# The delta rule's triangular inverse as 128-wide block diagonal matrices, and an mLSTM walk with zero padded operands

## The chip, the core and the metric

The kernel runs on one core of a Trainium2 chip. TensorE multiplies matrices, VectorE, ScalarE and GpSimd work on the results, and SyncE issues the DMAs. Measured is the device time of one execution, in microseconds; lower is better.

## The reference

One layer of a hybrid decoder, for a prompt of 256 tokens and 8 samples of one token each, with d_model 2048, all in fp32. An input projection of x feeds four mixers side by side: a gated delta rule (A, 8 heads), a Conformer convolution of width 31 (B), a short gated convolution (C) and an mLSTM matrix memory (D, 4 heads). Each is projected, gated and merged; then come an output projection, a cross-attention and a squared-ReLU MLP of 8192. What the change touches are the two recurrences, which run over the prompt in four chunks of 64 tokens:

```
# A, per chunk and head (L = 64)
a_low = where(strict, beta_i * (k k^T) * decay, 0)
sol   = triangular_solve(I + a_low, [v*beta, k*beta*exp(gc)])   # u, w
delta = u - w S;  o = q_dec S + (q k^T * decay) delta;  S = S*g_last + k_dec^T delta
# D, per chunk and head
dmat = exp(log_d - m_tok) * (q k^T)
num  = inter * (q C) + dmat v;  den = inter * (q n) + sum(dmat)
h    = num / max(|den|, exp(-m_tok))
C, n = scale * C + (k*wgt)^T v,  scale * n + k^T wgt
```

## The kernel before

Most of the work is weight matmuls. Every weight comes as blocks of 128x1024 (`raw`), is split into a high part `wh` (ScalarE) and a low part `wl` (VectorE, every second to fourth block GpSimd), and multiplied as wh*xh + wh*xl + wl*xh into `g` (L320). One block with its 24 matmuls is a *slot*; `run()` (L289) walks over all slots, feeds the blocks two slots ahead, and between slots pays out steps of two lists of generators: at most one step of `chain` (the delta units, row stage, mLSTM units) per slot and as many of `fill` (the convolution of B, 30 products per column block) as an estimate of VectorE's time, `dv_t` (L116), leaves room for. The order of instructions within each engine is settled when the program is built, by a scheduler with a timeline of its own.

The delta rule runs as four units of two heads (`a_unit`, L676). A unit normalises q and k, forms for four chunks and two heads the matrices A (strictly lower, scaled) and its transpose, and inverts I + A by doubling: T and U hold the inverse and its transpose for diagonal blocks of 2, and in five levels (L802, blocks of 2, 4, 8, 16, 32) X, minus the product of A and U, is formed in `xb`, evicted by ScalarE into `m_dl`, multiplied by T into `ub` and by the transpose into `tb`, and taken over by VectorE through a mask (`copy_predicated`, L818 and L821). Two chunks lie one above the other on the 128 partitions, each 64x64; `each()` (L655) issues eight 64x64 matmuls per product, which use a quarter of the array each. After the levels GpSimd copies U into the diagonal blocks of a zeroed 128x128 tile `UB` (L827), and the walk over the four chunks multiplies with that (`db`, `ob`, `sb`, `ks`, L844). Beside the levels, `side(li)` issues transposes and the sample part.

The mLSTM runs as two units of two heads (`d_unit`, L1074). Its walk (L1202) adds into one bank `nb` the product of the queries with C and that of the 64x64 matrices `QK` with v, head 0 in the output's lower 64 partitions and head 1 in the upper, and forms the update of C in `cb` from 64 rows of `kw` and v. The columns are 256 of v and one of ones, 257.

A matmul of fp32 operands shows as two records in the trace, one of fp32r operands (the weight matmuls) and a transpose as one.

Of the kernel before, what the change touches and what calls it, by code (L numbers as in the profile page):

```python
# [36 lines left out]
HP = 0  # L37
SCRATCH = 8192
DELAY = 3
# [52 lines left out]
def decoder_step(ctx, tc, A, O):  # L92
# [29 lines left out]
    def act(out, in_, func, bias=0.0, scale=1.0, **kw):  # L122
        return AC.activation(out, in_, func, bias=bias, scale=scale, **kw)  # L123

    def tt(out, a, b, op, eng=None):
        if eng is None:
            cost(out)
        return (eng or DV).tensor_tensor(out=out, in0=a, in1=b, op=op)  # L128

    def ts(out, a, s1, op0, s2=None, op1=None):  # L130
        cost(out, 0.6)
        if op1 is None:
            DV.tensor_scalar(out, a, s1, None, op0=op0)
        else:
            DV.tensor_scalar(out, a, s1, s2, op0=op0, op1=op1)
# [41 lines left out]
    cst = cp.tile([P, NCC], F32, name="cst")  # L177
    mint = cp.tile([P, 2, len(LEVELS), CH], mybir.dt.uint8, name="mint")
    oner = cp.tile([P, P], F32R, name="ones")
# [56 lines left out]
    def dma(dst, src):  # L236
        after(SP.dma_start(dst, src), "SP")
# [196 lines left out]
    selw = w1.tile([P, 8, P], F32R, name="selw")  # L434
    UB = w1.tile([P, 2, 2, P], F32, name="UB")
    dlz = [w1.tile([P, 2, P], F32, name="dl%d" % i) for i in range(2)]
    c1 = w1.tile([P, 2, 4, 8], F32, name="c1")
# [6 lines left out]
    GP.tensor_copy(RD[:].rearrange("p f l -> p (f l)"), zero[:].to_broadcast([P, 2 * CH]))  # L444
    GP.memset(UB[:], 0.0)
    for t in dlz:
        GP.memset(t[:], 0.0)
    rown = [0]
    nm = 2 * len(LEVELS) * CH
    w3 = rowt[:, 13:16, :]  # L450
    mf = w3.rearrange("p a b -> p (a b)")[:, 0:nm]

    ws = rowt[:, 4:6, :].rearrange("p a b -> p (a b)")[:, 0:32 * KB]

    def loads():
        dma(pc[:], A["pc"])
        dma(ws, A["ws"].rearrange("p k c -> p (k c)"))
        dma(cst[:], A["cst"])
        dma(mf, A["mint"].rearrange("p a b c -> p (a b c)"))
        win_a(0)  # L460
        win_b(0)
        dma(winC[:], A["sC"])
        dma(m0[rD, :], A["m0"])
# [16 lines left out]
    def row_stage():  # L480
        cp1, cp2 = rtile("cp1", NP), rtile("cp2", NP)
        GP.memset(cp1[:], 0.0)
        GP.memset(cp2[:], 0.0)
        cpy(mint[:].rearrange("p a b c -> p (a b c)"), mf)
        GP.memset(w3[:, 0, NP:], 0.0)
# [202 lines left out]
    def a_unit(u):  # L688
# [17 lines left out]
        sh = [P, 2, 2, CH]  # L706
        dL, dT = mat("m_dl"), mat("m_dt")
        Am, T, U = (mat("m_" + n) for n in ("a", "t", "u"))
        QK, X = dT, dL
        tt(dL[:], Gs[0], colb(c1, 1, h0, 2, sh), SUB)  # L710
        ts(dT[:], dL[:], 0.0, MIN)
        ts(dL[:], dL[:], 0.0, MAX)
        act(dT[:], dT[:], AF.Exp)
        act(dL[:], dL[:], AF.Exp, scale=-1.0)
        tt(U[:], KQ[:, :, :, 1, :], dT[:], MUL)
        tt(Am[:], KQ[:, :, :, 1, :], dL[:], MUL)
        tt(U[:], U[:], Gs[1], MUL)
        tt(dT[:], dT[:], con("incl")[:, None, None, :].to_broadcast(sh), MUL, eng=GP)
        tt(QK[:], KQ[:, :, :, 0, :], dT[:], MUL)
        yield  # L720
        tt(Am[:], Am[:], colb(c1, 0, h0, 2, sh), MUL)
        for dst, src, m in ((U, U, "m1u"), (T, Am, "m1t")):
            tt(dst[:], src[:], con(m)[:, None, None, :].to_broadcast(sh), MUL)
            tt(dst[:], dst[:], con("eye")[:, None, None, :].to_broadcast(sh), ADD)
        yield
        sv = [P, 2, 2, P]
        v5 = lambda b: b[:].rearrange("p (f h l) -> p f h l", f=2, h=2)
        vt, kd = (w1.tile(sv, F32, tag=n, name=n) for n in ("vt", "kd"))

        st = {}  # L730

        def side(li):
# [9 lines left out]
            if li == 1:  # L742
                kb = bank("kb")
                for i in range(4):
                    PE.transpose(kb[:, i * P:(i + 1) * P], k[:, i % 2, (i // 2) * P:(i // 2 + 1) * P], ident)
                tt(kd[:], v5(kb), colb(c1, 2, h0, 2, sv), MUL)
            if li == 2:
# [54 lines left out]
        for li, s in enumerate(LEVELS):  # L802
            last = li == len(LEVELS) - 1
            xb = v4(bank("xb"))
            for hf, hh, o, t in each():
                mm(xb[o, hf, hh], Am[o, hf, hh], U[o, hf, hh])
            act(X[:], xb, AF.Copy, scale=-1.0)
            side(li)
            yield
            ub = v4(bank("ub"))  # L810
            tb = None if last else v4(bank("tb"))
            for hf, hh, o, t in each():
                mm(ub[o, hf, hh], T[o, hf, hh], X[o, hf, hh])
            if not last:
                for hf, hh, o, t in each():
                    mm(tb[o, hf, hh], X[o, hf, hh], T[o, hf, hh])
            cost(U[:])
            DV.copy_predicated(U[:], mint[:, 0, li, None, None, :].to_broadcast(sh), ub)  # L818
            if not last:
                cost(T[:])  # L820
                DV.copy_predicated(T[:], mint[:, 1, li, None, None, :].to_broadcast(sh), tb)  # L821
            yield

        side(5)
        for c in range(2):
            o = slice(CH * c, CH * c + CH)
            GP.tensor_copy(UB[o, :, :, o], U[o])  # L827
        yield
# [18 lines left out]
        for c in range(NCH):  # L847
# [11 lines left out]
            for hh in range(2):  # L859
                mm(db[:, hh], UB[:, hf, hh], vt[:, hf, hh])  # L860
            act(dl[o], db[o], AF.Copy)
# [213 lines left out]
    def d_unit(u):  # L1075
# [3 lines left out]
        sh = [P, 2, 2, CH]  # L1079
        KQ = v4(bank("KQd"))  # L1080
# [3 lines left out]
        for hf, hh, o, t in each():  # L1084
            mm(KQ[o, hf, hh], k[:, hh, t], q[:, hh, t])
        E, QK = mat("m_dl"), mat("m_dt")
# [4 lines left out]
        tt(QK[:], KQ, E[:], MUL)  # L1091
        yield
# [11 lines left out]
        sv = [P, 2, 2, P]  # L1104
        kw = w1.tile(sv, F32, tag="kw", name="kwD")
        tt(kw[:], kb[:].rearrange("p (f h l) -> p f h l", f=2, h=2), colb(c2, 3, h0, 2, sv), MUL)
        yield
# [6 lines left out]
        for hh in range(2):  # L1114
            mm(ib[:, hh], sel(8 + h0 + hh, P), RR[:, 1, 0:NP])
        qi = q[:, :, 0:NP]
        tt(qi, q[:, :, 0:NP], ib, MUL)
        sl = w1.tile([P, 2, NCH], F32, tag="gl", name="sl")
# [83 lines left out]
        for c in range(NCH):  # L1202
            hf, o = c // 2, slice(CH * (c % 2), CH * (c % 2) + CH)
            t = slice(c * CH, c * CH + CH)
# [540 lines left out]
def _prep(i):  # L1745
# [43 lines left out]
    rst[:, ::CH] = 0.0  # L1789
    a["cst"] = np.concatenate([np.eye(P, dtype=f), (pl == j).astype(f), (pl <= j).astype(f), -up.astype(f), -lo.astype(f), rst], 1)  # L1790
    mi = np.zeros((P, 2, len(LEVELS), CH), np.float32)
    for n, s in enumerate(LEVELS):
        same = pl // (2 * s) == j // (2 * s)
        mi[:, 0, n] = same & (pl // s % 2 == 0) & (j // s % 2 == 1)
        mi[:, 1, n] = same & (pl // s % 2 == 1) & (j // s % 2 == 0)
    a["mint"] = mi
# [60 lines left out]
```

## Time and profile before

| | us |
|---|---|
| three runs | 2353.32, 2354.43, 2358.15 |
| median | 2354.43 |
| the profiled execution | 2356.15 |
| its span, first to last instruction | 2354.4 |

In the profile, "PE g L150" is a matmul into `g` recorded at line 150, the helper `mm`; PEld is the loading of its weights, DVE is VectorE, ACT ScalarE, POOL GpSimd. A shape such as "64*64 64x64" is the weights' rows and columns and the output's partitions and columns. A matmul's length in the timeline includes its way through the array, so that records overlap; what a stream costs is read from start to start. The rows of a timeline merge equal records ("x16") and show in brackets what the engine waited for.

### The profile page before, as it was taken

Reading aid. Unit: us, or ns where it says so; the run is one execution under the profiler, and the core shown is the slowest. Engines: PE = TensorE matmul, PEld = TensorE weight load, DVE = VectorE, ACT = ScalarE, POOL = GpSimd, SP = SyncE. Lnnn points to the kernel's source line nnn. Section 1 sums busy time; section 2 is a strip of 40 time slices with the busy share of each in tenths; the row PEclk is TensorE's granted clock in tenths of the full one; section 3 lists DMA queues with packets and bytes.
Section 4 is the critical chain, followed back from the end, with each engine's and each line's share of the span. In section 5 each row is a group of like instructions: output and inputs, shape, how many; then the busy total and the mean of one; then the engine's idle time right before and its main releaser. Section 6 shows DMA issues by size and latency. Waiting matters only on the chain.

```text
span 2354.4 us, 46439 instructions
## 1 busy us (share of the span) xinstructions
PE 2254.9 (96%) x19034; PEld 2210.5 (94%) x19034; DVE 1269.0 (54%) x2039; ACT 1166.9 (50%) x1789; POOL 978.9 (42%) x741
## 2 busy tenths in 40 slices
PE   9869999989999999999989999999999999999997
PEld 8869998988999999999989998889999999999997
DVE  7968899786446445443364466476323323323323
ACT  5735556545455455444434455456435534534543
POOL 3524435332122223343343355256445544544576
PEclk9989999999999999999999999999999999999998
DMA  6685555574566666766556666645666555556553
GB/s 228 161 121 169 168 168 163 162 136 146 176 185 194 185 217 201 226 193 181 180 181 180 190 204 196 202 145 156 180 180 179 179 180 179 179 180 180 179 180 126
DMA packets 140398, 418.78 MB, mean 178 GB/s; under 512 B 31896, under 2 KB 36248, under 8 KB 140184
## 3 DMA queue, kind: packets, MB, share of 16 engines
q1 hardware_dynamic: 140184, 415.80, 59.9%
q8 instruction: 149, 2.44, 0.4%
q14 instruction: 65, 0.53, 0.1%
HBM read 402.32 MB, written 14.38 MB: 177 GB/s over the span
## 4 chain that ended last, share of the span: by engine, by line
PE 77%; DVE 13%; DMA 5%; ACT 2%; issue 2%; POOL 1%; SPq 0%; DVEq 0%; POOLq 0%; ACTq 0%
PE g L150 70%; DVE wl L128 3%; DVE cB L139 3%; DMA raw<-in_win_dram 2%; DVE cu L139 2%; PE q L150 1%; DVE y L128 1%; PE pv L150 1%; DMA dbc<-dd 1%; ACT wh L123 1%; DMA mr<-in_memT_dram 1%; DVE y L139 1%; DMA raw<-in_winq_dram 1%; DVE s L139 0%; PE cb L150 0%
## 5 line engine op out<-in xcount | busy, mean ns | idle before, releaser
L123 ACT ACTIVATE wh<-raw 128x1024 fp32r<-128x1024 f32 (+1 forms) x705 | 745.3, 1058 | 850.3 <-PE g L150 283.1
L128 POOL TENSOR_TENSOR wl<-raw,wh 128x1024 fp32r<-128x1024 f32 x240 | 588.6, 2453 | 724.5 <-PE g L150 513.1
L150 PE MATMUL g<-xh,wl 128*128 128x264 f32 x2496 | 715.0, 287 | 11.4 <-DVE wl L128 8.8
L128 DVE TENSOR_TENSOR wl<-raw,wh 128x1024 fp32r<-128x1024 f32 (+1 forms) x465 | 588.5, 1266 | 253.0 <-PE g L150 166.7
L150 PE MATMUL g<-xh,wh 128*128 128x264 f32 x2496 | 717.6, 288 | 4.1 <-ACT wh L123 4.1
L150 PE MATMUL g<-xl,wh 128*128 128x264 f32 x2496 | 717.9, 288 | 1.3 <-issue 1.3
L150 PEld LDWEIGHTS g<-xh,wl 128*128 128x128 f32 x2496 | 473.9, 190 | 15.2 <-DVE wl L128 10.0
L150 PEld LDWEIGHTS g<-xh,wh 128*128 128x128 f32 x2496 | 474.4, 190 | 9.0 <-ACT wh L123 4.8
L150 PEld LDWEIGHTS g<-xl,wh 128*128 128x128 f32 x2496 | 473.1, 190 | 2.4 <-issue 1.5
L150 PE MATMUL g<-hgl,wh 128*128 128x264 f32 x1024 | 290.6, 284 | 0.0
L150 PE MATMUL g<-hgh,wl 128*128 128x264 f32 x1024 | 290.3, 284 | 0.0
L150 PE MATMUL g<-hgh,wh 128*128 128x264 f32 x1024 | 289.4, 283 | 0.0
L150 PE MATMUL g<-zh,wh 128*128 128x266 f32 x960 | 275.8, 287 | 2.4 <-DVE zw L128 2.4
L150 PE MATMUL g<-zl,wh 128*128 128x266 f32 x960 | 275.3, 287 | 0.0
L150 PE MATMUL g<-zh,wl 128*128 128x266 f32 x960 | 275.1, 287 | 0.0
L150 PEld LDWEIGHTS g<-hgl,wh 128*128 128x128 f32 x1024 | 192.9, 188 | 0.0
L150 PEld LDWEIGHTS g<-hgh,wh 128*128 128x128 f32 x1024 | 192.7, 188 | 0.0
L150 PEld LDWEIGHTS g<-hgh,wl 128*128 128x128 f32 x1024 | 192.0, 188 | 0.0
L150 PEld LDWEIGHTS g<-zh,wh 128*128 128x128 f32 x960 | 182.1, 190 | 2.5 <-ACT wh L123 2.5
L128 DVE TENSOR_TENSOR y<-y,g 128x264 f32<-128x264 f32 x80 | 34.3, 429 | 277.1 <-PE g L150 277.1
L150 PEld LDWEIGHTS g<-zl,wh 128*128 128x128 f32 x960 | 182.4, 190 | 0.0
L150 PEld LDWEIGHTS g<-zh,wl 128*128 128x128 f32 x960 | 181.6, 189 | 0.0
(482 smaller groups left out, 3453.5 us busy)
## 6 DMA issues: line engine op xcount, KB each, us to landing
raw<-in_win_dram SPq DMA_DIRECT2D x312, 512.0 KB, 4.1
raw<-in_f_dram SPq DMA_DIRECT2D x248, 512.0 KB, 4.2
raw<-in_wbr_dram SPq DMA_DIRECT2D x64, 512.0 KB, 3.7
raw<-in_wout_dram SPq DMA_DIRECT2D x32, 512.0 KB, 4.5
s<-in_sS_dram SPq DMA_DIRECT2D x8, 512.0 KB, 5.6
dbc<-dd SPq DMA_DIRECT2D x16, 256.0 KB, 3.7
out_S_s_dram<-s SPq DMA_DIRECT2D x8, 512.0 KB, 5.1
c<-in_sCm_dram SPq DMA_DIRECT2D x8, 512.0 KB, 5.3
```

The source lines that it names most:

```text
L123: return AC.activation(out, in_, func, bias=bias, scale=scale, **kw)
L128: return (eng or DV).tensor_tensor(out=out, in0=a, in1=b, op=op)
L139: return DV.scalar_tensor_tensor(out=out, in0=a, scalar=s, in1=b, op0=op0, op1=op1)
L150: PE.matmul(out, lhsT, rhs, start=start, stop=stop)
```

## The change

All matrices of the inverse (A, T, U, X) become 128x128 per pair of chunks, with the two 64x64 matrices on the diagonal and zeros beside them, in one tile `inv` that lives through all units; each product is four 128x128 matmuls instead of eight 64x64 ones. U is then multiplied directly, and UB and its copies go. The masks are twice as wide and come as bytes, without the cast. In the mLSTM, `KQd` is formed for whole 128-token pairs, `QK`, `qi` and `kw` are written into zeroed parts of `inv` and a tile `walk` (in every row 64 zeros, then the other head's 64 columns), so that each matmul of the walk uses 128 rows and writes 128 output partitions, and both heads add into the same bank.

```diff
-    UB = w1.tile([P, 2, 2, P], F32, name="UB")
-    dlz = [w1.tile([P, 2, P], F32, name="dl%d" % i) for i in range(2)]
+    inv = w1.tile([P, 4, 2, 2, P], F32, name="inv")
+    walk = w1.tile([P, 4, 2, P], F32, name="walk")
+    Am, T, U, X = (inv[:, i] for i in range(4))
+    dlz = [walk[:, 2 + i] for i in range(2)]
...
-        dma(mf, A["mint"].rearrange("p a b c -> p (a b c)"))
+        dma(mint[:], A["mint"])
...
-        cpy(mint[:].rearrange("p a b c -> p (a b c)"), mf)
... a_unit
-        tt(Am[:], Am[:], colb(c1, 0, h0, 2, sh), MUL)
-        for dst, src, m in ((U, U, "m1u"), (T, Am, "m1t")):
-            tt(dst[:], src[:], con(m)[:, None, None, :].to_broadcast(sh), MUL)
-            tt(dst[:], dst[:], con("eye")[:, None, None, :].to_broadcast(sh), ADD)
+        for c in range(2):
+            o = slice(CH * c, CH * c + CH)
+            tt(Am[o, :, :, o], Ah[o], colb(c1[o], 0, h0, 2, [CH, 2, 2, CH]), MUL)
+        sb = [P, 4, P]
+        f4 = lambda t: t.rearrange("p f h l -> p (f h) l")
+        Uv = f4(Uh)[:, :, None, :].to_broadcast([P, 4, 2, CH])
+        tt(f4(U).rearrange("p g (s l) -> p g s l", s=2), Uv,
+           con("m1u").rearrange("p (s l) -> p s l", s=2)[:, None].to_broadcast([P, 4, 2, CH]), MUL)
+        tt(f4(T), f4(Am), con("m1t")[:, None, :].to_broadcast(sb), MUL)
+        for t in (U, T):
+            tt(f4(t), f4(t), ident[:, None, :].to_broadcast(sb), ADD)
...
-            xb = v4(bank("xb"))
-            for hf, hh, o, t in each():
-                mm(xb[o, hf, hh], Am[o, hf, hh], U[o, hf, hh])
-            act(X[:], xb, AF.Copy, scale=-1.0)
+            xb = v5(bank("xb"))
+            for hf, hh in pairs:
+                mm(xb[:, hf, hh], Am[:, hf, hh], U[:, hf, hh])
+            act(X, xb, AF.Copy, scale=-1.0)
...
-            for hf, hh, o, t in each():
-                mm(ub[o, hf, hh], T[o, hf, hh], X[o, hf, hh])
+            for hf, hh in pairs:
+                mm(ub[:, hf, hh], T[:, hf, hh], X[:, hf, hh])
...
-            DV.copy_predicated(U[:], mint[:, 0, li, None, None, :].to_broadcast(sh), ub)
+            DV.copy_predicated(U, mint[:, 0, li, None, None, :].to_broadcast(sv), ub)
...
-        for c in range(2):
-            o = slice(CH * c, CH * c + CH)
-            GP.tensor_copy(UB[o, :, :, o], U[o])
...
-                mm(db[:, hh], UB[:, hf, hh], vt[:, hf, hh])
+                mm(db[:, hh], U[:, hf, hh], vt[:, hf, hh])
... d_begin
+            GP.memset(inv[:, 0:2], 0.0)
+            GP.memset(inv[:, 2:4], 0.0)
+            GP.memset(walk[:], 0.0)
... d_unit
-        for hf, hh, o, t in each():
-            mm(KQ[o, hf, hh], k[:, hh, t], q[:, hh, t])
+        for hf in range(2):
+            for hh in range(2):
+                t = slice(hf * P, hf * P + P)
+                mm(KQ[:, hf, hh], k[:, hh, t], q[:, hh, t])
...
-                    mm(nb[64 * hh:64 * hh + 64, :257], qi[:, hh, t], C[:, hh, :], stop=False)
+                    mm(nb[:, :257], qi[:, c, CH * hh:CH * hh + P], C[:, hh, :], start=hh == 0, stop=False)
             for hh in range(2):
-                mm(nb[64 * hh:64 * hh + 64, :257], QK[o, hf, hh], vt[o, hf, hh, :], start=c == 0)
+                mm(nb[:, :257], QK[:, hf, c % 2, CH * hh:CH * hh + P], vt[:, hf, hh, :], start=c == 0 and hh == 0, stop=hh == 1)
...
-                mm(cbs[hh], kw[o, hf, hh], vt[o, hf, hh])
+                mm(cbs[hh], kw[:, hf, c % 2, hh], vt[:, hf, hh])
```

On TensorE, in the first delta unit, the second level before, between the weight matmuls `g` (`kb` are transposes of `side`; `m_a`, `m_u`, `m_dl`, `m_t` are A, U, X and T):

```order
L150 MATMUL g<-xl,wh 128x264
L150 MATMUL xb<-m_u,m_a 64x64 x8
L745 MATMUL kb<-cst,qkv 128x128 x4
L150 MATMUL g<-xh,wl 128x264
...
L150 MATMUL g<-xh,wh 128x264
L150 MATMUL ub<-m_dl,m_t 64x64 x8
L150 MATMUL tb<-m_t,m_dl 64x64 x8
L150 MATMUL g<-xl,wh 128x264
```

The same level now, with all four matrices in `inv`:

```order
L150 MATMUL g<-xh,wh 128x264
L150 MATMUL xb<-inv 128x128 x4
L753 MATMUL kb<-cst,qkv 128x128 x4
L150 MATMUL g<-xl,wh 128x264
...
L150 MATMUL g<-xh,wh 128x264
L150 MATMUL ub<-inv 128x128 x4
L150 MATMUL tb<-inv 128x128 x4
L150 MATMUL g<-xl,wh 128x264
```

Half as many matmuls of four times the area stand at the same place; no weight matmul moves between them.

On TensorE, the second chunk of the first mLSTM unit's walk before (`hb` transposes the chunk before it, `C` is the matrix memory):

```order
L150 MATMUL g<-xh,wl 128x264
L1236 MATMUL hb<-cst,hs 128x128 x2
L150 MATMUL nb<-C,qkvD 64x257 x2
L150 MATMUL nb<-vtD,m_dt 64x257 x2
L150 MATMUL cb<-vtD,kwD 128x257 x2
L150 MATMUL g<-xh,wh 128x264
```

and now:

```order
L150 MATMUL g<-xh,wl 128x264
L1253 MATMUL hb<-cst,hs 128x128 x2
L150 MATMUL nb<-C,walk 128x257 x2
L150 MATMUL nb<-vtD,inv 128x257 x2
L150 MATMUL cb<-vtD,inv 128x257 x2
L150 MATMUL g<-xh,wh 128x264
```

The number of matmuls and their place are the same; the two products into `nb` have 128 output partitions instead of 64.

On ScalarE, in the first delta unit, an eviction of X between the weight blocks before (`cB`, `ht` and `cuC` belong to the two convolutions):

```order
L123 ACTIVATE cB<-extB,pc 128x256
L123 ACTIVATE ht<-g,pc 128x264
L123 ACTIVATE wh<-raw 128x1024 x2
L123 ACTIVATE m_dl<-xb 128x256
L123 ACTIVATE wh<-raw 128x1024
L123 ACTIVATE cuC<-extC,pc 128x256
```

and now:

```order
L123 ACTIVATE cB<-extB,pc 128x256
L123 ACTIVATE ht<-g,pc 128x264
L123 ACTIVATE wh<-raw 128x1024 x2
L123 ACTIVATE inv<-xb 128x512
L123 ACTIVATE wh<-raw 128x1024
L123 ACTIVATE cuC<-extC,pc 128x256
```

It is the eviction of the third level before and of the second now; it stands behind the same two weight blocks, and is twice as wide.

## Rows read from the trace of the kernel before

**Rows 1.** The page: busy us (share of span) and instructions by engine

```profile
PE 2254.9 (96%) x19034; PEld 2210.5 (94%) x19034; DVE 1269.0 (54%) x2039; ACT 1166.9 (50%) x1789; POOL 978.9 (42%) x741
```

**Rows 2.** Two stretches: PE, PEld, DVE, ACT, POOL busy us, clock, DMA share, GB/s

```profile
150.00:500.00 350.00, 334.76 (x3142) 324.85 (x3140) 310.86 (x550) 189.11 (x344) 143.78 (x177) 1.00 0.54 165
...
640.00:1200.00 560.00, 560.00 (x4592) 545.32 (x4591) 267.49 (x419) 272.56 (x392) 167.30 (x96) 1.00 0.64 194
```

**Rows 3.** TensorE's timeline, fourth unit, first level: start, length, instruction

```profile
553.74 0.28 PE L150 MATMUL g<-xh,wh 128*128 128x264 f32 x1
553.95 0.68 PE L150 MATMUL ub<-m_dl,m_t 64*64 64x64 f32 x16
554.47 0.63 PE L150 MATMUL tb<-m_t,m_dl 64*64 64x64 f32 x16
555.03 0.39 PE L150 MATMUL g<-xl,wh 128*128 128x264 f32 x1
555.25 0.28 PE L150 MATMUL g<-xh,wl 128*128 128x264 f32 x1
```

**Rows 4.** The same timeline, last level of the first unit

```profile
175.62 0.28 PE L150 MATMUL g<-xh,wh 128*128 128x264 f32 x1
175.84 0.68 PE L150 MATMUL ub<-m_dl,m_t 64*64 64x64 f32 x16
...
176.67 0.28 PE L150 MATMUL g<-xh,wl 128*128 128x264 f32 x1
```

**Rows 5.** The same timeline, ks of the fourth unit

```profile
595.47 0.28 PE L150 MATMUL g<-pairC,wh 128*128 128x264 f32 x1
595.59 0.61 PE L150 MATMUL ks<-S,qkv 128*128 128x128 f32 x4
...
596.16 0.29 PE L150 MATMUL g<-pairC,wl 128*128 128x264 f32 x1
```

**Rows 6.** The same timeline, second chunk of the first mLSTM unit

```profile
825.02 0.28 PE L150 MATMUL g<-xh,wl 128*128 128x264 f32 x1
...
825.45 0.65 PE L150 MATMUL nb<-C,qkvD 128*64 128x257 f32 x4
826.03 0.65 PE L150 MATMUL nb<-vtD,m_dt 64*64 64x257 f32 x4
826.62 1.13 PE L150 MATMUL cb<-vtD,kwD 64*128 64x257 f32 x4
...
827.91 0.29 PE L150 MATMUL g<-xl,wh 128*128 128x264 f32 x1
```

**Rows 7.** The same timeline, attention product of 256 columns

```profile
1542.78 0.28 PE L150 MATMUL gxo<-ox,wl 128*128 128x264 f32 x1
1542.90 1.46 PE L150 MATMUL av<-att 128*128 128x256 f32 x6
...
1544.44 0.29 PE L150 MATMUL gxo<-ox,wl 128*128 128x264 f32 x1
```

**Rows 8.** VectorE's groups, 50 to 600 us: count, busy us, mean ns, idle before

```profile
L818 DVE COPY_PREDICATED m_u<-mint,ub 128x256 f32<-128x256 uint8 x20 | 8.9, 443 | 6.5 <-PE ub L150 6.5
...
L128 DVE TENSOR_TENSOR vt<-vb,c 128x512 f32<-128x512 f32 x4 | 2.7, 682 | 0.6 <-PE vb L740 0.6
...
L128 DVE TENSOR_TENSOR m_t<-m_t,cst 128x256 f32<-128x256 f32 x4 | 1.7, 413 | 0.0
```

**Rows 9.** GpSimd's groups: a memset

```profile
L445 POOL MEMSET UB<- 128x512 f32 x1 | 0.5, 524 | 0.0
```

**Rows 10.** The page: what the DMA engines moved

```profile
DMA packets 140398, 418.78 MB, mean 178 GB/s; under 512 B 31896, under 2 KB 36248, under 8 KB 140184
```

**Rows 11.** TensorE's waits, 100 to 600 us: total, times, longest

```profile
PE ub L150 <- ACT m_dl L123: 15.7, 1, 15.7
PE ssl2q L150 <- ACT sql2q L123: 4.2, 2, 2.6
...
PE ssl2q L150 <- POOL sql2q L128: 0.4, 1, 0.4
```

More of the change, by code (lines that the diff above doesn't have):

```diff
@@ L37 @@
 HP = 0
-SCRATCH = 8192
+SCRATCH = 4096
 DELAY = 3
@@ L84 @@
 _n = 0
-for _name, _w in (("ident", 128), ("eye", 64), ("incl", 64), ("m1u", 64), ("m1t", 64), ("reset", 256)):
+for _name, _w in (("ident", 128), ("incl", 64), ("m1u", 128), ("m1t", 128), ("reset", 256)):
     _cc[_name] = (_n, _w)
@@ L177, in decoder_step @@
     cst = cp.tile([P, NCC], F32, name="cst")
-    mint = cp.tile([P, 2, len(LEVELS), CH], mybir.dt.uint8, name="mint")
+    mint = cp.tile([P, 2, len(LEVELS), P], mybir.dt.uint8, name="mint")
     oner = cp.tile([P, P], F32R, name="ones")
@@ L444, in decoder_step @@
     GP.tensor_copy(RD[:].rearrange("p f l -> p (f l)"), zero[:].to_broadcast([P, 2 * CH]))
-    GP.memset(UB[:], 0.0)
-    for t in dlz:
-        GP.memset(t[:], 0.0)
+    GP.memset(Am, 0.0)
+    GP.memset(walk[:, 2:4], 0.0)
     rown = [0]
-    nm = 2 * len(LEVELS) * CH
     w3 = rowt[:, 13:16, :]
-    mf = w3.rearrange("p a b -> p (a b)")[:, 0:nm]
     ws = rowt[:, 4:6, :].rearrange("p a b -> p (a b)")[:, 0:32 * KB]
@@ L706, in a_unit @@
         sh = [P, 2, 2, CH]
[L707 to L712, printed above, removed]
+        QK = dT = mat("m_dt")
+        pairs = [(hf, hh) for hf in range(2) for hh in range(2)]
+        xv = X.rearrange("p f h l -> p (f h l)").rearrange("p (s f h l) -> p s f h l", s=2, f=2, h=2)
+        dL, Uh = xv[:, 0], xv[:, 1]
+        Ah = U.rearrange("p f h l -> p (f h l)")[:, :256].rearrange("p (f h l) -> p f h l", f=2, h=2)
+        tt(dL, Gs[0], colb(c1, 1, h0, 2, sh), SUB)
+        ts(dT[:], dL, 0.0, MIN)
+        ts(dL, dL, 0.0, MAX)
         act(dT[:], dT[:], AF.Exp)
[L714 to L717, printed above, removed]
+        act(dL, dL, AF.Exp, scale=-1.0)
+        tt(Uh, KQ[:, :, :, 1, :], dT[:], MUL)
+        tt(Ah, KQ[:, :, :, 1, :], dL, MUL)
+        tt(Uh, Uh, Gs[1], MUL)
         tt(dT[:], dT[:], con("incl")[:, None, None, :].to_broadcast(sh), MUL, eng=GP)
@@ L727, in a_unit @@
         v5 = lambda b: b[:].rearrange("p (f h l) -> p f h l", f=2, h=2)
-        vt, kd = (w1.tile(sv, F32, tag=n, name=n) for n in ("vt", "kd"))
+        vt = w1.tile(sv, F32, tag="vt", name="vt")
+        kd = walk[:, 0:2]
         st = {}
@@ L745, in side @@
                     PE.transpose(kb[:, i * P:(i + 1) * P], k[:, i % 2, (i // 2) * P:(i // 2 + 1) * P], ident)
-                tt(kd[:], v5(kb), colb(c1, 2, h0, 2, sv), MUL)
+                tt(kd, v5(kb), colb(c1, 2, h0, 2, sv), MUL)
             if li == 2:
@@ L803, in a_unit @@
             last = li == len(LEVELS) - 1
-            xb = v4(bank("xb"))
-            for hf, hh, o, t in each():
-                mm(xb[o, hf, hh], Am[o, hf, hh], U[o, hf, hh])
-            act(X[:], xb, AF.Copy, scale=-1.0)
+            xb = v5(bank("xb"))
+            for hf, hh in pairs:
+                mm(xb[:, hf, hh], Am[:, hf, hh], U[:, hf, hh])
+            act(X, xb, AF.Copy, scale=-1.0)
             side(li)
             yield
-            ub = v4(bank("ub"))
-            tb = None if last else v4(bank("tb"))
-            for hf, hh, o, t in each():
-                mm(ub[o, hf, hh], T[o, hf, hh], X[o, hf, hh])
+            ub = v5(bank("ub"))
+            tb = None if last else v5(bank("tb"))
+            for hf, hh in pairs:
+                mm(ub[:, hf, hh], T[:, hf, hh], X[:, hf, hh])
             if not last:
-                for hf, hh, o, t in each():
-                    mm(tb[o, hf, hh], X[o, hf, hh], T[o, hf, hh])
-            cost(U[:])
-            DV.copy_predicated(U[:], mint[:, 0, li, None, None, :].to_broadcast(sh), ub)
+                for hf, hh in pairs:
+                    mm(tb[:, hf, hh], X[:, hf, hh], T[:, hf, hh])
+            cost(U)
+            DV.copy_predicated(U, mint[:, 0, li, None, None, :].to_broadcast(sv), ub)
             if not last:
-                cost(T[:])
-                DV.copy_predicated(T[:], mint[:, 1, li, None, None, :].to_broadcast(sh), tb)
+                cost(T)
+                DV.copy_predicated(T, mint[:, 1, li, None, None, :].to_broadcast(sv), tb)
             yield
         side(5)
-        for c in range(2):
-            o = slice(CH * c, CH * c + CH)
-            GP.tensor_copy(UB[o, :, :, o], U[o])
         yield
@@ L1079, in d_unit @@
         sh = [P, 2, 2, CH]
-        KQ = v4(bank("KQd"))
+        KQ = bank("KQd")[:].rearrange("p (f h l) -> p f h l", f=2, h=2)
+        flat = inv[:].rearrange("p a f h l -> p (a f h l)")
+        kw = flat[:, 0:1024].rearrange("p (f c h l) -> p f c h l", f=2, c=2, h=2)
+        QK = flat[:, 1024:1792].rearrange("p (f c z) -> p f c z", f=2, c=2)
+        qi = walk[:].rearrange("p a h l -> p (a h l)")[:, :768].rearrange("p (c z) -> p c z", c=NCH)
+        spread = lambda t: t.rearrange("p f (h l) -> p f h l", h=3)[:, :, 0:3:2, :]
         G = bank("Gd")[:, :256].rearrange("p (h f l) -> p h f l", h=2, f=2)
@@ L1083, in d_unit @@
             mm(G[:, hh], selc(h0 + hh), RD[:])
-        for hf, hh, o, t in each():
-            mm(KQ[o, hf, hh], k[:, hh, t], q[:, hh, t])
-        E, QK = mat("m_dl"), mat("m_dt")
+        for hf in range(2):
+            for hh in range(2):
+                t = slice(hf * P, hf * P + P)
+                mm(KQ[:, hf, hh], k[:, hh, t], q[:, hh, t])
+        E = mat("m_dt")
         tt(E[:], G.rearrange("p h f l -> p f h l"), colb(c1, 3, h0, 2, sh), SUB)
@@ L1090, in d_unit @@
         tt(E[:], E[:], con("incl")[:, None, None, :].to_broadcast(sh), MUL)
-        tt(QK[:], KQ, E[:], MUL)
+        for c in range(2):
+            o = slice(CH * c, CH * c + CH)
+            tt(spread(QK[o, :, c]), KQ[o, :, :, o], E[o], MUL)
         yield
@@ L1104, in d_unit @@
         sv = [P, 2, 2, P]
-        kw = w1.tile(sv, F32, tag="kw", name="kwD")
-        tt(kw[:], kb[:].rearrange("p (f h l) -> p f h l", f=2, h=2), colb(c2, 3, h0, 2, sv), MUL)
+        for c in range(2):
+            o = slice(CH * c, CH * c + CH)
+            tt(kw[o, :, c], kb[o].rearrange("p (f h l) -> p f h l", f=2, h=2), colb(c2[o], 3, h0, 2, [CH, 2, 2, P]), MUL)
         yield
@@ L1115, in d_unit @@
             mm(ib[:, hh], sel(8 + h0 + hh, P), RR[:, 1, 0:NP])
-        qi = q[:, :, 0:NP]
-        tt(qi, q[:, :, 0:NP], ib, MUL)
+        ph = lambda t: t.rearrange("p h (c l) -> p c h l", l=CH)
+        tt(spread(qi), ph(q[:, :, 0:NP]), ph(ib), MUL)
         sl = w1.tile([P, 2, NCH], F32, tag="gl", name="sl")
@@ L1202, in d_unit @@
         for c in range(NCH):
-            hf, o = c // 2, slice(CH * (c % 2), CH * (c % 2) + CH)
-            t = slice(c * CH, c * CH + CH)
+            hf, t = c // 2, slice(c * CH, c * CH + CH)
             nb = bank("nb")
@@ L1789, in _prep @@
     rst[:, ::CH] = 0.0
-    a["cst"] = np.concatenate([np.eye(P, dtype=f), (pl == j).astype(f), (pl <= j).astype(f), -up.astype(f), -lo.astype(f), rst], 1)
-    mi = np.zeros((P, 2, len(LEVELS), CH), np.float32)
+    own = p // CH == np.arange(P)[None] // CH
+    bd = lambda m: (np.concatenate([m, m], 1) & own)
+    a["cst"] = np.concatenate([np.eye(P, dtype=f), (pl <= j).astype(f), -bd(up).astype(f), -bd(lo).astype(f), rst], 1)
+    mi = np.zeros((P, 2, len(LEVELS), P), np.uint8)
     for n, s in enumerate(LEVELS):
         same = pl // (2 * s) == j // (2 * s)
-        mi[:, 0, n] = same & (pl // s % 2 == 0) & (j // s % 2 == 1)
-        mi[:, 1, n] = same & (pl // s % 2 == 1) & (j // s % 2 == 0)
+        mi[:, 0, n] = bd(same & (pl // s % 2 == 0) & (j // s % 2 == 1))
+        mi[:, 1, n] = bd(same & (pl // s % 2 == 1) & (j // s % 2 == 0))
     a["mint"] = mi
```

## The prediction

> **What bounds the kernel now.** I read the busy shares first, then the stretches, and in the stretches that the change touches TensorE's own timeline and its waits. The reader should see that TensorE is busy 96% of the span [rows 1]. From 150 to 500 us, where three of the four delta units run, it is busy 334.76 of 350 us and VectorE 310.86, at full clock; from 640 to 1200 us, where both mLSTM units run, it has no gap at all [rows 2]. So a microsecond added to TensorE's own work is a microsecond on the path in the mLSTM stretch, and nearly so among the delta units, as long as it doesn't fall into a wait that something else ends.
>
> The small matmuls stand in the stream of weight matmuls (g), which start 0.12 us apart. What a group of them costs is therefore the time from the start of the last g before it to the start of the second g behind it, less two steps of 0.12 us; this takes in whatever a change of tile shape costs in front and behind. The groups ub and tb of one level together: 555.25 - 553.74 = 1.51, less 0.24, is 1.27 us [rows 3]. A lone group of 16 records of 64x64: 176.67 - 175.62 = 1.05, less 0.24, is 0.81 us [rows 4].
>
> **The change part by part.** *The five levels.* Each group of eight 64x64 fp32 matmuls (16 records) becomes four of 128x128 moving 128 columns (8 records). The trace has that very form: ks, 4 records, takes 596.16 - 595.47 = 0.69, less 0.24, which is 0.45 us or 0.1125 per record, with full-array work on both sides [rows 5]. A group after the change costs 8 x 0.1125 = 0.90 us. Four units of five levels make 20 groups of xb, 20 of ub and, without the last level, 16 of tb.
> - ub with tb: 1.80 instead of 1.27, 16 x 0.53 = +8.5 us.
> - lone ub: 0.90 instead of 0.81, 4 x 0.09 = +0.4 us.
> - xb has the form of the lone ub, but full-array products stand right behind it, so its switch back is shared; I take 0.78 (an estimate: 0.81 of [rows 4] less a little): 20 x 0.12 = +2.4 us.
>
> Together +11.3 us. What the change saves here, the switching of tile shape, is inside these differences already: ub starts 553.95 - 553.74 = 0.21 behind the last g instead of 0.12, and 555.25 is 0.22 behind the g that follows tb [rows 3].
>
> The Trainium skill speaks for the change in one place. "TensorEngine Tiling (Array Packing)", Key Properties, says that a change of tiling mode drains the engine. The rows agree: some 0.1 us in front of a group and 0.1 behind it [rows 3]. By the rule alone, with what the groups stream left as it is, the levels' 40 places in the stream would gain 40 x 0.2 = 8 us instead of losing 11.
>
> *The mLSTM walk.* A middle chunk from hb on: 827.91 - 825.02 = 2.89, less 0.24, is 2.65 us [rows 6]. Afterwards hb keeps its two records (0.225), and nb and cb are 12 records of 257 columns on the whole array. A record of 256 columns costs (1544.44 - 1542.78 - 3 x 0.12) / 6 = 0.217 us [rows 7]; I take 0.22 for 257. So 0.225 + 12 x 0.22 = 2.87, +0.22 us, six times: +1.3 us. The first chunk of a unit is nb and cb alone: 826.62 - 826.03 = 0.59 and 827.91 - 826.62 less one step, 1.17, together 1.76 [rows 6], and 8 x 0.22 = 1.76 afterwards: nothing. The product KQd goes from 16 records of 64 wide tiles to 8 full ones, which the lone ub prices at +0.1, twice: +0.2 us.
>
> *VectorE.* The 36 predicated copies go from 256 to 512 elements. A 128x256 one takes 0.443 us, and the step from 256 to 512 elements is 0.682 - 0.413 = 0.27 us in two-operand operations [rows 8]. That is 36 x 0.27 = 9.7 us; two masks, two additions of the identity and the splitting of one multiplication add 4 x 0.27 + 0.41 = 1.5 us per unit, 6.0 in all: 15.7 us more while the delta units run. At nothing: VectorE had 39 us free between 150 and 500 and is half idle from 640 on [rows 2], and the planner puts the steps of the convolution, which fill what is left, later when it counts more work. If that cover fails, all of it is on the path: 0 to 15.7, taken as 0, since TensorE slows by a similar share and so leaves VectorE the time.
>
> *The other engines.* ScalarE evicts X as 512 instead of 256 elements, 20 times some 0.27 us more (an estimate, by the step of [rows 8]), on an engine busy 189 of 350 us [rows 2]: 0 to 5 on the path, taken as 0. GpSimd loses eight copies into UB, and gets three memsets of 1024 elements at the start of the mLSTM part, some 1 us each by 0.524 for 512 [rows 9]; behind them one low part wl can be late, 0 to 1 us, taken as 0. The mask arrives as bytes, 160 instead of 320 KB, the constants grow by 32 KB; 128 KB less at the mean of 178 GB/s [rows 10] are 0.7 us: -0.7 to 0, taken as 0.
>
> *Order.* The planner pays at most one step of a unit per slot. In the new order unit 0 begins its levels a slot later, closes a gap at the fourth level and then runs up to three slots ahead; the others run one to three slots ahead and end where they did. So waits fall elsewhere. The largest, 15.7 us of ub for ScalarE, is the arrival of a weight block behind which the eviction of X is queued [rows 11]; it stays, since an eviction of X still stands behind two weight blocks there. Ten rows of waits for a unit's own results, from 4.2 to 0.4 us, sum to 22.2 [rows 11]; I leave them as they are, between all of them gone and 10 us more.
>
> Sum: 11.3 + 1.3 + 0.2 = +12.8 us. The profiled execution took 2356.15 us (span 2354.4), 1.7 above the median of 2354.43; so 2369 for such an execution, and 2367 for the median.
>
> **The rivals.**
> *VectorE becomes the bound.* Its 15.7 us come on top, because the predicated copies stand between one level and the next and the same engine makes the low parts of the weights: +28.5 us, 2383. For it: 89% busy, and TensorE already waits for it. Against it: the 39 us that it was idle in that stretch.
> *The waits give some back.* The UB copies leave GpSimd's queue and units run ahead, so 8 to 17 of the 22.2 us go; with 12.8 of them the time is 2354.
> *Faster.* The same mechanism in full: TensorE stops waiting for its units' results, -22.2 us, 2345. It decides from 17.5 us on (12.8 and the 4.7 of no change). Against it: most of these waits are for VectorE, which gets more work, not less.
> *The switches are the price of the small tiles.* Then the levels gain 0.2 us in each of 40 places, 8 us [rows 3], with the walk -6.5, 2348. Against it: ks, which fixes what a full-array record streams. It is the rule of the Trainium skill, "TensorEngine Tiling (Array Packing)", Key Properties, taken alone.
> *The small tiles ran side by side.* If the four quadrants worked at once, the 0.52 us from ub to tb [rows 3] stand for a quarter of the work, and a group would become 2.1 us: 56 x 1.2 = 67 us more than the forecast, 2434. Against it: two groups like ks make one new group, at 0.90. The Trainium skill, same page, Theoretical Speedup, gives up to a factor of 2 for each small dimension, which is where this rival comes from; ks shows a doubling, not four times.
> *The change does not do what it says.* KQ of the delta units keeps its 64-wide outputs and so its switches, four times in all; it is the same before and after.
>
> **How the numbers follow.** The forecast 0.62, with its own range of +8 to +18 us (2362 to 2372); VectorE as the bound, wholly or in part, 0.15; no change by returned waits 0.13; faster by waits 0.06, by switches 0.02; side by side 0.02. Within 0.2%, or 4.7 us, is about what a measurement of this kernel can tell from no change. So slower 0.79, same 0.13, faster 0.08. The range of 2353 to 2383 leaves out most of the faster cases, the far end of VectorE's and the last rival.
>
> **What would show it.** In the new profile a ub with its tb should take about 1.8 us between weight matmuls and xb 0.9; a middle mLSTM chunk 2.87 from hb on; a predicated copy 0.71; TensorE's waits should sum to what they do now. If ub with tb costs 1.3 or less, the price per record is wrong; if it costs 1.8 and the total stays, the waits were it; if the total rises by over 25, TensorE's waits for VectorE in the first 600 us should have grown by as much.

## The result and the profile after

| | before | after |
|---|---|---|
| median of the runs shown, us | 2353.88 | 2375.16 |
| lowest to highest, us | 2352.18 to 2358.15 | 2373.28 to 2380.17 |
| span of the profiled execution, us | 2354.4 | 2371.5 |

The changed kernel is slower: ratio 1.0091, 95% interval 1.0070 to 1.0112, or 21.4 us (16.5 to 26.4). The forecast was +12.8, with +8 to +18 as its own range. The direction and the price of the matmuls came out; some 8 us are not in the sum, and the measured median lies above that range, inside the wider one of 2353 to 2383.

The busy shares, the answer to [rows 1]:

```profile
PE 2273.7 (96%) x18570; PEld 2244.5 (95%) x18570; DVE 1284.5 (54%) x2046; ACT 1168.1 (49%) x1786; POOL 972.4 (41%) x735
```

TensorE is 18.8 us busier than in [rows 1], with 464 records fewer, and VectorE 15.5. The time in which TensorE does nothing is what it was: 2371.5 - 2273.7 = 97.8 us, before 2354.4 - 2254.9 = 99.5. So in this pair of executions the loss lies in matmuls that take longer, not in longer waits. (Their spans are 17.1 us apart, the medians 21.3: a pair of executions shows where time went, and its size only roughly.) The same two stretches as in [rows 2] (columns as there):

```profile
150.00:500.00 350.00, 332.75 (x2772) 326.62 (x2770) 303.35 (x531) 185.19 (x332) 127.91 (x165) 0.99 0.51 155
640.00:1200.00 560.00, 560.00 (x4567) 552.88 (x4566) 270.97 (x422) 272.56 (x391) 171.71 (x100) 1.00 0.63 195
```

In a fixed stretch the later work is pushed out, which is why VectorE reads lower here although it has more to do; the second stretch still has no gap on TensorE. TensorE's timeline at the places of [rows 3, 4]: a `ub` with its `tb` in the fourth unit, then the lone `ub` of the first unit's last level (start, length, instruction).

```profile
571.80 0.28 PE L150 MATMUL g<-xh,wl 128*128 128x264 f32 x1
571.92 1.05 PE L150 MATMUL ub<-inv 128*128 128x128 f32 x8
572.81 1.06 PE L150 MATMUL tb<-inv 128*128 128x128 f32 x8
573.62 0.37 PE L150 MATMUL g<-xh,wh 128*128 128x264 f32 x1
573.83 0.29 PE L150 MATMUL g<-xl,wh 128*128 128x264 f32 x1
...
171.44 0.29 PE L150 MATMUL g<-xh,wh 128*128 128x264 f32 x1
171.56 1.06 PE L150 MATMUL ub<-inv 128*128 128x128 f32 x8
...
172.58 0.28 PE L150 MATMUL g<-xh,wl 128*128 128x264 f32 x1
```

573.83 - 571.80 - 0.24 = 1.79 us against 1.27, and 172.58 - 171.44 - 0.24 = 0.90 against 0.81. `ub` now starts 0.12 behind the last g, as a g does: the extra step in front of the group is gone, the longer stream costs more than that. The step behind the group stays: 573.83 - 573.62 = 0.21, where [rows 3] have 0.22. An `xb` with the product `eb` behind it, in the fourth unit, first before and then after:

```profile
564.76 0.28 PE L150 MATMUL g<-xh,wh 128*128 128x264 f32 x1
564.97 0.68 PE L150 MATMUL xb<-m_u,m_a 64*64 64x64 f32 x16
...
566.04 0.28 PE L150 MATMUL g<-xh,wl 128*128 128x264 f32 x1
```

The same in the kernel after:

```profile
575.90 0.28 PE L150 MATMUL g<-xh,wh 128*128 128x264 f32 x1
576.02 1.05 PE L150 MATMUL xb<-inv 128*128 128x128 f32 x8
...
577.27 0.29 PE L150 MATMUL g<-xh,wl 128*128 128x264 f32 x1
```

1.28 becomes 1.37, +0.09, with 0.12 in the sum. The second chunk of the first mLSTM unit, the answer to [rows 6]:

```profile
844.44 0.28 PE L150 MATMUL g<-xh,wl 128*128 128x264 f32 x1
844.56 0.38 PE L1253 MATMUL hb<-cst,hs 128*128 128x128 f32 x2
844.78 1.03 PE L150 MATMUL nb<-C,walk 128*128 128x257 f32 x4
...
847.51 0.28 PE L150 MATMUL g<-xl,wh 128*128 128x264 f32 x1
```

847.51 - 844.44 - 0.24 = 2.83 us against 2.65, and 2.87 in the forecast. TensorE's waits from 100 to 600 us, the answer to [rows 11] (total, times, longest):

```profile
PE ub L150 <- ACT inv L123: 18.1, 2, 17.4
PE KQ L150 <- DVE qkv L128: 11.0, 2, 9.3
```

These two are the places where a weight block comes late behind a long store (experiment 4). The first is 1.7 us longer. What follows it on TensorE:

```profile
143.53 2.08 PE L150 MATMUL ub<-inv 128*128 128x128 f32 x8 [17.41 <-ACT inv L123]
145.40 1.91 PE L150 MATMUL tb<-inv 128*128 128x128 f32 x8
146.97 0.57 PE L150 MATMUL g<-xl,wh 128*128 128x264 f32 x1
147.33 0.42 PE L150 MATMUL g<-xh,wl 128*128 128x264 f32 x1
147.55 0.42 PE L150 MATMUL g<-xh,wh 128*128 128x264 f32 x1
```

Behind the wait the g start 0.22 us apart instead of 0.12, and from the start of `ub` to the second g behind `tb` it is 147.33 - 143.53 = 3.80 us, twice the 573.83 - 571.92 = 1.91 of above. The window of this stretch gives the granted clock (the number before the DMA share):

```profile
143.60:147.20 3.60, 3.60 (x17) 3.60 (x18) 3.53 (x8) 1.33 (x2) 1.38 (x2) 0.50 0.41 146
```

0.50 is the lower of its two levels, 1.2 GHz, after a wait of 17.4 us in which TensorE did nothing, and 1.00 the upper. So a matmul that lands behind such a wait is paid twice, and the change has made the matmuls that land there longer. Over the span the mean granted clock is 0.985 before and 0.982 after. Summed over all stretches of the span at 0.50, first before, then after (us, then busy us by engine as in [rows 2], and the means of a stretch):

```profile
sum 72.80, PE 39.54 PEld 38.80 DVE 52.51 ACT 35.90 POOL 22.27; mean PE 3.59 PEld 3.53 DVE 4.77 ACT 3.26 POOL 2.02
sum 85.63, PE 49.98 PEld 49.66 DVE 64.01 ACT 42.92 POOL 23.72; mean PE 3.57 PEld 3.55 DVE 4.57 ACT 3.07 POOL 1.69
```

A matmul there takes twice its time, so half of TensorE's busy time in them is the price of the lower clock: 19.8 us before and 25.0 after. Of the 18.8 us that TensorE is busier, an estimated 5.2 are clock and 13.6 are work, for which the sum had 12.8. (The kernels of this document with the same matmuls differ by up to some 4 us in what is left when that half is taken off.) The Trainium skill, "TensorE: Matmul & The Clock Gate", HAM oscillation, describes a matmul stream that falls to the slow clock behind each wait for a transfer; the trace agrees, with 3.80 against 1.91 us here. VectorE's copies (count, busy us, mean ns, idle before), against [rows 8], where `ub`'s took 443 ns:

```profile
L826 DVE COPY_PREDICATED inv<-mint,ub 128x512 f32<-128x512 uint8 x20 | 14.7, 733 | 9.8 <-PE ub L150 9.6
L829 DVE COPY_PREDICATED inv<-mint,tb 128x512 f32<-128x512 uint8 x16 | 11.7, 733 | 0.6 <-PE tb L150 0.6
```

0.733 against 0.443 us, +0.29 each where the sum had 0.27.

### The profile page after: what moved, and what is told of

Same layout as the page of the kernel before. It is cut to its first block, busy times and chain, and to the rows that moved or that the text cites. A ratio compares the mean times of both kernels' runs of the same rounds, so it can differ in the third digit from the quotient of the medians.

```text
span 2371.5 us, 45499 instructions
## 1 busy us (share of the span) xinstructions
PE 2273.7 (96%) x18570; PEld 2244.5 (95%) x18570; DVE 1284.5 (54%) x2046; ACT 1168.1 (49%) x1786; POOL 972.4 (41%) x735
## 4 chain that ended last, share of the span: by engine, by line
PE 78%; DVE 12%; DMA 3%; issue 3%; ACT 2%; POOL 1%; SPq 0%; DVEq 0%; ACTq 0%; POOLq 0%
PE g L150 70%; DMA raw<-in_win_dram 2%; DVE wl L128 2%; DVE cB L139 2%; DVE cu L139 2%; PE q L150 1%; DVE y L128 1%; PE pv L150 1%; ACT wh L123 1%; DVE y L139 1%; DVE inv L128 1%; DVE s L139 1%; PE ub L150 1%; PE nb L150 1%; PE xb L150 1%
```

## The experiments

Three theories for the 8 us above the price of the matmuls: **V**, VectorE's added work, costed at nothing, reaches TensorE; **S**, the two late weight blocks are met at a worse place; **O**, the planner's changed order costs by itself. Ratios are to runs of the kernel before on the same chip; microseconds are the ratio less 1 times its median there (2346.5 to 2353.9).

The change also halves `SCRATCH`, the program's scratch for DMAs, from 8192 to 4096. That wasn't tried apart. The padded walk alone (experiment 1) and the runs with VectorE's work alone (experiment 2 and the first of 6) have it halved too; the walk with it measured +1.9 us, at most 4.2 by its interval, which leaves it little.

**1. The two halves apart.** The kernel after with the mLSTM part of before; the delta units, `inv` and the byte masks stay as in the kernel after:

```diff
-                    mm(nb[:, :257], qi[:, c, CH * hh:CH * hh + P], C[:, hh, :], start=hh == 0, stop=False)
+                    mm(nb[64 * hh:64 * hh + 64, :257], qi[:, hh, t], C[:, hh, :], stop=False)
...
```

> The levels in 128-wide matrices, the mLSTM as before. Theory of the price (TensorE pays per record, the mLSTM part is worth 1.3 us): 18 to 21 us over the kernel before, 1 to 2 below the changed one. Rival (the mLSTM's padding costs more than its records, by its extra copies and memsets): under 16 over the kernel before.

Measured 1.0082 (1.0067 to 1.0097), +19.2 us. And the levels of before with the padded walk:

```diff
-                    mm(nb[64 * hh:64 * hh + 64, :257], qi[:, hh, t], C[:, hh, :], stop=False)
+                    mm(nb[:, :257], qi[:, c, CH * hh:CH * hh + P], C[:, hh, :], start=hh == 0, stop=False)
...
```

> The padded mLSTM walk, the levels as before (the zeroed tiles lie over UB, the dl pair and kd to fit). Price: +0.5 to +2.5 us, a middle chunk of 2.83 instead of 2.65 us between weight matmuls. Rival: +5 us or more, with new waits between 780 and 1010 us.

Measured 1.0008 (0.9999 to 1.0018), +1.9 us. The halves add up to 21.1 against 21.4, so nothing that these runs can tell is owed to their meeting; the excess is in the delta units.

**2. VectorE's work alone.** The kernel before with 56 operations more on VectorE, whose result nobody uses:

```diff
+        def more(n):
+            for _ in range(n):
+                ts(junk[:], Am[:].rearrange("p f h l -> p (f h l)"), 0.0, MAX)
+        more(5)
...
             DV.copy_predicated(U[:], mint[:, 0, li, None, None, :].to_broadcast(sh), ub)
+            more(1)
...
                 DV.copy_predicated(T[:], mint[:, 1, li, None, None, :].to_broadcast(sh), tb)
+                more(1)
```

> The kernel before with VectorE's added work alone: one product of 256 elements (0.28 us, result unused) behind each of the 36 predicated copies and five before the levels of each unit, 56 x 0.28 = 15.7 us. If VectorE's added work made the 8 to 9 us beyond the price: +6 to +16 us. If it is covered: within 3 us of the kernel before.

Measured 1.0026 (1.0016 to 1.0037), +6.1 us. The group of them:

```profile
L133 DVE TENSOR_SCALAR junk<-m_a 128x256 f32<-128x256 f32 x56 | 22.1, 395 | 0.4
```

They took 22.1 us, not the 15.7 planned, so the end came later by 28% of them: the lower edge of what theory V had. The planner counted them and moved the levels, so this run doesn't tell the work from the order (experiment 5).

**3. TensorE's work alone.** The kernel before with transposes and 64 records of full 128x128 products behind the levels' groups:

```diff
+            PE.transpose(xbk[:, 256:384], ident, ident)
...
+                for i in range(2):
+                    mm(tbk[:, 256 + 128 * i:384 + 128 * i], ident, ident)
```

> The kernel before with TensorE's added work alone: one transpose of the identity (0.11 us) in each of 20 xb groups and two 128x128 fp32 products (4 records, 0.45 us) behind each of 16 tb groups, results unused: 9.4 us. Price theory: +8 to +12 us. If VectorE bounds the delta units: under +4 us.

Measured 1.0065 (1.0050 to 1.0080), +15.3 us, above what the price has. In its timeline the added records cost what was meant:

```profile
548.49 0.71 PE L150 MATMUL tb<-cst 128*128 128x128 f32 x4
548.95 0.37 PE L150 MATMUL g<-xh,wh 128*128 128x264 f32 x1
```

`tb`'s extra four records are 548.95 - 548.49 = 0.46. So some 6 us (2 to 9 by the interval) came from elsewhere, with no work on VectorE added. The scheduler also moved the later units' levels up to 3.8 slots earlier here, and up to 4.7 in experiment 2, which made theory O.

**4. The stalls.** The long store is a copy of the convolution's state from memory to memory. In the kernel before, a weight block issued 1.9 us behind it took 29.1 us to land, where the block issued just before the store took 6.7, and ScalarE waited for it:

```profile
141.56 1.06 ACT L123 ACTIVATE wh<-raw 128x1024 fp32r<-128x1024 f32 x1 [19.75 <-DMA raw<-in_win_dram]
```

The store's row among the DMA issues of the kernel before (count, KB each, us to landing), with that of the second late store:

```profile
out_gl_s_dram<-in_sB_dram SPq DMA_DIRECT2D x1, 928.0 KB, 30.2
...
out_gl_s_dram<-gcs SPq DMA_DIRECT2D x1, 32.0 KB, 17.5
```

and both cut into eight pieces, one behind each column block:

```profile
out_gl_s_dram<-in_sB_dram SPq DMA_DIRECT2D x8, 116.0 KB, 7.4
...
out_gl_s_dram<-gcs SPq DMA_DIRECT2D x8, 4.0 KB, 4.7
```

```diff
-                store(O["gl_s"][:, :, :, 0:29], A["sB"][:, :, :, 1:30])
+            store(O["gl_s"][:, j, :, 0:29], A["sB"][:, j, :, 1:30])
...
-            if j == NB - 1:
-                store(O["gl_s"][:, :, :, 29], gcs[:])
+            store(O["gl_s"][:, j, :, 29], gcs[:, j, :])
```

In the kernel before:

> The kernel before, with its two late stores of the convolution's state cut into eight pieces, one behind each column block, so that no single long transfer holds up the weight blocks. Both theories: the 15.7 us wait of ub for ScalarE and the two waits near 521 us go, so 8 to 20 us faster than the kernel before, 2330 to 2345.

Measured 0.9938 (0.9925 to 0.9952), -14.5 us: faster than both kernels. In the kernel after:

> The kernel after with the same cut. Theory S (the part of the loss above the price on TensorE, some 8 us, comes from the two stalls on late weight blocks, which the changed order meets at a worse place): it stands only 10 to 14 us above the split kernel before, so it gains about 8 us more from the cut than before does. Theory V (the excess is VectorE's added 15.7 us, a part of which is on the path wherever the weights come in time): the distance stays at 18 to 23 us.

Measured 1.0016 (1.0007 to 1.0025), +3.8 us. The distance between the two is 18.3 us (about 3.8 either way, the two intervals combined): theory V's number, and little below the 21.4 with the stalls in. Both large waits are gone; what TensorE waits for in the cut kernel after, 100 to 620 us:

```profile
PE xb L150 <- DVE inv L128: 3.9, 3, 2.8
...
PE ub L150 <- ACT inv L123: 1.3, 1, 1.3
...
PE KQ L150 <- DVE qkv L128: 0.3, 1, 0.3
```

Theory S is left with some 3 us (21.4 less 18.3), and these are within the uncertainty.

**5. The order.** The kernel before, the planner counting VectorE's work as in the kernel after:

```diff
+        dv_t[0] += 4 * 0.27 + 0.34
...
-            cost(U[:])
+            cost(U[:], 2.0)
...
```

> The kernel before, with the planner counting VectorE's work as the kernel after does (about 0.3 us more per copy and level): the same instructions, only in the order that the larger numbers give. Theory O (a changed order alone costs, whatever the work): +4 to +10 us. Theories V and S: within 3 us of the kernel before.

Measured 1.0029 (1.0017 to 1.0040), +6.8 us: theory O's number, with not one instruction added. Its mean granted clock is 0.983, against 0.985 in the kernel before. At the second stall it has one wait, where before had three of 2.4 to 3.0 us:

```profile
530.26 1.98 PE L150 MATMUL KQ<-qkv 128*64 128x128 f32 x16 [7.10 <-DVE qkv L128]
```

`KQ` behind it runs at the lower clock, 1.98 us long. The same order with the cut stores:

> The split kernel before, with the planner's larger counts: only the order differs from the split kernel before. Theory O in general (an order away from the tuned one costs wherever it is): +4 to +8 us above the split kernel before, 2337 to 2341. Theory O by the stalls (the changed order only meets the long stores at a worse place): within 2 us of it.

Measured 0.9935 (0.9922 to 0.9947), against 0.9938 for the cut kernel before: no difference. This order costs where it meets the long stores, and nothing that can be measured without them. Now the other way round, the work of after in an order nearer to before's:

```diff
-BACK = 3.0
+BACK = 4.0
...
+        dv_t[0] -= 1.42
...
-            cost(U)
+            cost(U[:, 0])
...
```

> The kernel after, its planner counting the copies and products as the kernel before does, with 4.0 instead of 3.0 us of slack: the work is that of the kernel after, and from the third delta unit's start on the order lies within two slots of that of before, where after's runs one to three slots ahead. Theory O (above the 12.8 us of work on TensorE, after pays some 7 us for its changed order): 13 to 16 us above the kernel before. Theory V (it pays for VectorE's added work): 19 to 23 above.

Measured 1.0080 (1.0066 to 1.0094), +18.8 us (15.5 to 22.1): just under theory V's range, above theory O's, and clear neither of it nor of the 21.4. With the cut stores as well:

> The kernel after with before's counts and the stores cut into eight pieces, in an order within two slots of that of before. Theory O: 10 to 15 us above the split kernel before (2333), so 2343 to 2348, and 2 to 7 us faster than the split kernel after in its own order. Theory V: as the split kernel after, 2350.

Measured 1.0031 (1.0019 to 1.0042), +7.3 us, 21.8 above the cut kernel before and 3.5 slower than the cut kernel after in its own order (some 3 either way). In both runs the planner counts VectorE's longer copies short, which costs by itself (experiment 6), so alone they don't decide. With the cut stores, where an order like after's cost nothing, the distance is still 18.3; so theory O falls as the cause of the loss.

**6. VectorE's work, uncounted and taken away.** Experiment 2 again, not told to the planner:

```diff
-                ts(junk[:], Am[:].rearrange("p f h l -> p (f h l)"), 0.0, MAX)
+                DV.tensor_scalar(junk[:], Am[:].rearrange("p f h l -> p (f h l)"), 0.0, None, op0=MAX)
```

> The kernel before with the same 56 unused operations on VectorE as in the experiment on VectorE alone (15.7 us), but not counted by the planner: the order stays within two slots of before. Theory O (the earlier 6 us were the changed order): 0 to +3 us. Theory V (they were the work): +5 to +8 us.

Measured 1.0059 (1.0046 to 1.0073), +13.8 us, more than any theory had. The operations:

```profile
L724 DVE TENSOR_SCALAR junk<-m_a 128x256 f32<-128x256 f32 x56 | 19.9, 356 | 0.5
```

13.8 of 19.9 us, 69%, came through in an order within two slots of before's. Counted by the planner it was 28%, with a change of order in it; that putting the convolution's steps later absorbed the rest is likely, and not shown apart. Last, the cut kernel after with half of each copy, so that half of the inverse is never updated:

```diff
-            DV.copy_predicated(U, mint[:, 0, li, None, None, :].to_broadcast(sv), ub)
+            DV.copy_predicated(U[:, 0], mint[:, 0, li, None, :].to_broadcast([P, 2, P]), ub[:, 0])
...
-                DV.copy_predicated(T, mint[:, 1, li, None, None, :].to_broadcast(sv), tb)
+                DV.copy_predicated(T[:, 0], mint[:, 1, li, None, :].to_broadcast([P, 2, P]), tb[:, 0])
```

> The split kernel after, each of the 36 predicated copies taking 256 of the 512 elements: half of the matrices of the inverse are not updated, the number of instructions and what they wait for are as before, and VectorE has 9.7 us less. Theory V (a third to all of VectorE's added work reaches TensorE): 3 to 9 us faster than the split kernel after (2349.8, ratio 1.0016), so 0.9978 to 1.0004 of the kernel before. Theory P (VectorE's copies are covered, and what stands above the 12.8 us is something else): within 2 us of the split kernel after.

Measured 0.9982 (0.9973 to 0.9992), -4.2 us, so 8.0 us (about 3 either way) below the cut kernel after. The copies:

```profile
L826 DVE COPY_PREDICATED inv<-mint,ub 128x256 f32<-128x256 uint8 x20 | 8.9, 444 | 9.4 <-PE ub L150 9.4
L829 DVE COPY_PREDICATED inv<-mint,tb 128x256 f32<-128x256 uint8 x16 | 7.1, 445 | 2.8 <-PE tb L150 2.7
```

36 x 0.29 = 10.4 us less on VectorE gave 8.0 back. The third unit's levels also came up to 1.6 slots earlier; in experiment 5 larger moves cost nothing with the stores cut. What is left, 10.3 us (about 4 either way) above the cut kernel before, is about the price on TensorE. Where the 8 us show is told by the page of the cut kernel after, and then of this one:

```profile
PE 2272.3 (97%) x18570; PEld 2242.5 (96%) x18570; DVE 1283.8 (55%) x2046; ACT 1166.7 (50%) x1786; POOL 971.9 (41%) x735
```

```profile
PE 2265.8 (97%) x18570; PEld 2236.3 (96%) x18570; DVE 1279.9 (55%) x2046; ACT 1166.7 (50%) x1786; POOL 977.0 (42%) x735
```

With the same matmuls TensorE is 6.5 us less busy; its idle time (spans 2345.8 and 2341.0) is 73.5 and 75.2 us, and its mean granted clock rises from 0.988 to 0.990. In this pair of executions the shorter copies bought matmuls at the higher clock, not shorter waits. The pair is a weak witness: it is 4.8 us apart and not 8.0, the eleven runs of the cut kernel after have mean clocks of 0.986 to 0.990 and the twelve of this one 0.988 to 0.990, and of the 6.0 us less that the lower clock costs here (reckoned as at the top) 2.0 lie behind 1200 us, where no such copy runs. In the first run of this experiment VectorE's work shows as waiting instead: TensorE is busy 2255.3 us of a span of 2356.4, so idle 101.1, against 91.3 (2347.8 less 2256.5) in the padded walk alone, on another chip and in before's order. That VectorE's work reaches the end time is shown; how much of it comes as lower clock and how much as longer waits is not.

## Why the prediction was right, and what it missed

*The levels and the walk on TensorE (+12.8).* Right to within about 1 us. By the rows of after: `ub` with `tb` 16 x 0.52 = 8.3, the lone `ub` 4 x 0.09 = 0.4, `xb` 20 x about 0.1 = 2, the middle mLSTM chunks 6 x 0.18 = 1.1: 11.8 us before KQd, and 13.6 by the busy time above. The padded walk alone measured +1.9 us, with 1.5 in the sum. That ks prices a full-array record carried the whole term, and put an end to two rivals: the group of four streams 0.90 us, neither quicker for the lost switches nor twice as long as the small tiles side by side would have had it. The step in front of `ub` did go from 0.21 to 0.12. The Trainium skill, "TensorEngine Tiling (Array Packing)", Key Properties, says that a change of tiling mode drains the engine; the trace agrees, with 0.21 against 0.12 in front of a group, which is the smaller part of the change. The prediction also put the 0.22 behind the group down to the switch; it is still 0.21 after, so the 40 places are worth 40 x 0.09 = 3.6 us, and not the 8 that the rival of the switches was given.

*VectorE at nothing.* This step failed. Its size was about right (15.5 us more busy, 15.7 in the sum, though so close a match is in part luck: the same work read 1283.8 us in the cut kernel after and 1295.5 in the other order), its cover was not. Of the 39 us in which VectorE stood idle [rows 2] a part lies where it waits for TensorE's `ub` (6.5 us before [rows 8], 9.6 after, over 50 to 600 us), and no further step of the same chain can fill that; this reason is argued, the failure of the cover is measured. Of work added there 28% came through when the planner could move the convolution for it and 69% when it couldn't, and of the copies' 10.4 us, taken away again, 8.0 (5 to 11) came back. By these shares 4 to 12 of the 15.5 us were on the path; the gap to be explained is 8 to 9. The rival that VectorE becomes the bound, "wholly or in part", described this, and had 0.15 where its partial form should have been the forecast.

*Waits left as they are.* The idle time did stay (99.5 and 97.8 us), though not wait by wait: `KQ` grew to 9.3 us where three shorter waits had stood. What the prediction had no term for is what a wait does to the matmuls behind it: 5.2 us of lower clock in this pair. The order by itself cost 6.8 us beside the long stores and nothing without them. How much of that the kernel after pays is not resolved: 21.4 with the stores whole, 18.3 with them cut, 18.8 in an order nearer to before's, each 3 to 5 us uncertain.

*The other costs at nothing.* ScalarE, GpSimd and the mask were not tried apart; with 12 to 14 of price and 8 of VectorE's copies, little is left for them.

Open is experiment 3: 6 us above its own 9.4 us of TensorE work. In its trace they are idle time of TensorE: 2358.8 us of span less 2260.6 busy is 98.2 us, against the 91.3 of the padded walk alone, in before's order on the same chip. A changed order beside the stalls can do that much, as experiment 5 shows, but it wasn't tried with the stores cut. The last run of experiment 6 speaks for it: with the stores cut and the copies short, the whole matmul work of the change cost 10.3 us and no surplus.

The version to keep from these runs is the kernel before with its two stores cut, ratio 0.9938 to before, in either order; against the kernel after it is 0.9938 / 1.0091, some 1.5% faster.

## What to carry to other kernels

Zeros in a matrix are not free on a full array: price the wider matmul by a row of the same form elsewhere in the trace, start to start, and set the saved switch against it. Idle time on a helper engine covers added work only if that work can go there; where the engine is idle because it waits in the same chain, cost the work at half to most of its length (here 69 and 77% came through, and 28% where the planner could move other work for it). Before reading a few microseconds out of an order, look for a long transfer that the order meets; here cutting two stores into eight pieces each gained 14.5 us, two thirds of what the whole change under study cost.

## What was not expected of the hardware

A store of 928 KB from memory to memory took 30.2 us, one of 32 KB took 17.5, and a weight block behind the first took 29.1; in eight pieces the stores took 7.4 and 4.7 us each, and the kernel became 14.5 us shorter. The same VectorE operation took 395 ns in one order and 356 in another.
